# MLP turns by transfers, a scheduler with a backward pass, and another opening for head 0, in a retention and latent-attention decoder

## The chip, the cores and the metric

The kernel runs on one core of one Trainium2 chip. The metric is the time of one execution on the device in microseconds (us), as the median of three runs. One further execution was taken with the hardware profiler; every trace row below is from that one. The engines are named as the profile names them: PE (TensorE, the matrix products), PEld (its weight loads), DVE (VectorE), ACT (ScalarE), POOL (GpSimd) and SP (SyncE, which issues most of the transfers).

## The reference, cut to what matters

The input x has 256 tokens of 2048 features. One retention layer (8 heads, queries and keys of 256, gates and values of 512 columns) and one latent-attention layer follow each other, each with a squared-ReLU MLP of 8192 hidden columns behind it.

```python
h = rms_norm(x, norm_mix[0]);  x = x + retention(h, ret_w_in, ret_w_out, cos, sin)
x = x + square(relu(rms_norm(x, norm_mlp[0]) @ w1[0])) @ w2[0]
k_nope, k_pe, v = mla_shared_kv(rms_norm(x, kv_norm_in), ...)   # the latent: 2048 -> 512 + 64, then up
x = x + mla_attention(rms_norm(x, norm_mix[1]), ..., k_nope, k_pe, v)
x = x + square(relu(rms_norm(x, norm_mlp[1]) @ w1[1])) @ w2[1]
```

In a head of retention, `q` and `k` are rotated by cos and sin of the positions, `o = (q k^T * decay) v`, and `silu(gate) * o / rms(o)` goes into the output projection. All data is float32.

## The kernel before, in words

**Products.** Every float32 operand is split into a high part (rounded to float32r, by ACT, tiles `*_wh` for weights) and a low part (what is left, by DVE, `*_wl`), and a product is three matrix products: high x high, high x low, low x high. Weights are streamed in chunks of up to 1 MB into three `raw` buffers, issued by SP; the split tiles have five buffers each (`wh`, `wl`).

**Pairs.** Most projections go by `gemm_pair` (L812): two column blocks of 512 together, in chunks of 256 rows. A chunk is a 2 x 2 block product, done with eight block products (24 matrix products) or, where `kinds` says so, with seven (21), after the manner of Strassen. A seven-product chunk needs sums of weights and of activations, which DVE makes (`*_u`, `*_sum`, `*_more`). Tuples such as SEVEN, ODD, LATE and HEAD name the chunks with seven. A pair fills four accumulator banks (`acc`), two of tag `tp` and the double bank `at`; `pair_out` (L853) copies them out. Queries and keys go by `gemm_t` (L729), plain columns by `gemm` (L891).

**Turning.** The next product needs its input transposed, with the features on the partitions. Two ways exist. On PE: `transposed` (L649), a product of 128 columns with the identity for each 128 x 128 block, into a `tp` bank. By transfer: `turn_by_dma` (L660), where ACT copies each block's 16-bit halves apart (`*_h`), SP issues four transposing transfers per block pair (`*_t`), and `joined` (L676) puts the halves together on ACT.

**The MLP.** `mlp` (L1296) works in four groups. In a group, two up pairs (p even, p odd) make hidden blocks 0 to 3 and 4 to 7, then two down pairs (`d_.0`, `d_.1`) use these eight blocks as chunks 0 to 7. `up` scales and applies the ReLU (ACT), turns, squares (ACT) and splits. STEPS (L466) says how: blocks of the even pair are turned by transfer, those of the odd pair (`None`) on PE, in `turn_on_pe` (L1308). The even pair's blocks have the odd pair's time to get ready; the odd pair's blocks are used from the fifth chunk of the first down pair on.

**The opening.** Head 0 starts with its gate column (`rg`), then queries (`rq`), keys (`rk`) and its value column (`rv`), while x arrives block by block in `start` (L1119). POOL computes angles for the rotation in `sincos` (L995), one chain of 512 columns for retention (`tr`), one of 128 for the latent layer (`tm`); ACT takes the sine (`tr_sc`), DVE scales it by the tokens' rstd, and PE turns it (`tr_tp`) into `rope_tab`. All later heads do queries, keys and then gates and values as one pair (`rp`). The output projection `ro` comes in two halves, after heads 3 and 7; TURNED_Y (L463) says up to which head the results y are turned by transfer.

**Order.** The program is first recorded as a list of operations (`Plan`, L125), with times estimated by a table. `due_dates` (L229) goes back once over the dependencies, and `schedule` (L255) goes forward over the engines, taking on each the ready operation that is due first. Queue order on every engine, DMA issues included, comes from that. In every engine's queue the instructions start in that order: a waiting one holds those behind it.

Of the kernel before, what the change touches and what calls it, by code (L numbers as in the profile page):

```python
# [23 lines left out]

AHEAD = {"f2k": 25000, "act": 30000, "small": 60000}
# [99 lines left out]
class Plan:  # L125
# [129 lines left out]
    def schedule(self):  # L255
        import heapq

        self.due_dates()
        free = dict.fromkeys(self.LATENCY, 0.0)
# [7 lines left out]
        blocked = {t: {} for t in self.tags}  # L267
        for op in self.ops:
# [219 lines left out]
def yoco(ctx: ExitStack, tc: tile.TileContext, a):  # L488
# [49 lines left out]
    cst = nc.tile(pool, [P, C_ALL], F32, "cst")  # L538
# [3 lines left out]
    ident = cst[:, C_ID : C_ID + P]  # L542
    mask = cst[:, C_MASK : C_MASK + 3 * P]
# [8 lines left out]
    for i in range(9):  # L552
        nc.tensor.matmul(idle, zeros[:, 0:P], zeros, start=i == 0, stop=i == 8)
# [128 lines left out]
    def stream(w, chunk, cols, name, use, done=None, before=None):  # L682
# [5 lines left out]
        for half in range(2):  # L688
# [3 lines left out]
            if before is not None:  # L692
                cuts = 1 if half and chunk else 2
# [15 lines left out]
    def piece(w, chunk, acc, act, g, nk, nb, name, before=None, done=None):  # L709

        if before is None:
            need(act, 2 * g + 2)

        def use(half, wh, wl):
# [9 lines left out]
        stream(  # L724
            w, chunk, 4 * nb, f"{name}{g}", use, done and (lambda: done(acc)),
            before and (lambda half: before(2 * g + half)),
        )

    def gemm_t(w, chunk0, act, nk, name, done):  # L729
# [3 lines left out]
        for g in range(n):  # L733
            need(act, 4 * g + 4)

            def use(half, wh, wl):
                for j in range(4):
                    k = g * 8 + half * 4 + j
                    a = act[k // 2][:, k % 2]
                    for f in range(2):  # L740
                        cols = slice(j * 256 + f * P, j * 256 + (f + 1) * P)

                        def low():
                            nc.tensor.matmul(acc[f][:, 0:S], wl[:, cols], a[:, 0], start=False, stop=False)

                        if k > 0:
                            low()
                        nc.tensor.matmul(
                            acc[f], wh[:, cols], a.rearrange("p i s -> p (i s)"), start=k == 0, stop=k == nk - 1
                        )  # L750
                        if k == 0:
                            low()

            stream(w, chunk0 + g, 2048, f"{name}{g}", use, (lambda: done(acc)) if g == n - 1 else None)
# [136 lines left out]
    def gemm(w, chunk0, act, nk, nb, name, done, before=None):  # L891
# [3 lines left out]
        for g in range(n - 1):  # L895
            piece(w, chunk0 + g, acc, act, g, nk, nb, name, before)
        last_piece(w, chunk0, acc, act, nk, nb, name, done, before)

    def last_piece(w, chunk0, acc, act, nk, nb, name, done, before=None):
        g = nk // 4 - 1  # L900
        piece(w, chunk0 + g, acc, act, g, nk, nb, name, before, done)
# [143 lines left out]
    def mla_tables():  # L1045
        sm = mla_sc[0](no_turn[0])
# [14 lines left out]
    def ret_tables():  # L1061
        nc.vector.tensor_copy(pos_f, pos_i)
        ret_sc.append(sincos(cst[:, C_INVR : C_INVR + 128], 128, "tr"))

    def scale_tables():
# [3 lines left out]
        no_turn.append(zero)  # L1069
        sc = ret_sc[0](zero)  # L1070
        scaled = f2k([2, NT, P], "tr_scaled")
        for t in range(NT):
            nc.vector.tensor_scalar(scaled[:, :, t], sc[:, :, t], r0[t], None, op0=ALU.mult)
# [4 lines left out]
        later(1, turn)  # L1078


    act0, sums0, r0, ret_sc, mla_sc, no_turn = [], [], [], [], [], []
# [673 lines left out]
```

## Time and profile before

| | us |
|---|---|
| runs | 2434.78, 2441.07, 2440.16 |
| median | 2440.16 |
| profiled execution | 2433.66 |
| its span, first to last instruction | 2431.9 |
| PE, DVE, ACT, POOL busy | 2415.1, 2228.8, 1764.0, 251.7 |

A row of the chain or of the timeline gives the start, the duration, the engine, and what is done, with its count after the x. Where it ends in square brackets, the engine sat idle for that long before it, until the engine and tile named had finished. A group's row gives the busy time of the group, the mean of one in ns, and the idle time before them. A stretch gives busy time and count of each engine between two times, PE's clock, the busy share of the DMA engines and GB/s. In the names, what is written stands left of the arrow; the trace leaves buffer numbers out.

### The profile page before, as it was taken

The numbers are of one execution on the slowest core, as the hardware profiler recorded it, in microseconds if no ns is written. First come the engines' busy times: TensorE is split into PE (matmuls) and PEld (weight loads), VectorE is DVE, ScalarE is ACT, GpSimd is POOL, SyncE is SP. The second block draws the span as 40 slices with busy tenths as digits, with TensorE's granted clock in tenths as the row PEclk, the third lists the DMA queues.
The fourth block names the chain that finished last, engine by engine and source line by source line (L and its number), as shares of the span: only waits on it lengthen the run. The fifth ranks groups of instructions, "written<-read, shape, count | busy, mean of one in ns | idle before, by whom it ended". The sixth has DMA issues, their size and how long they took to land.

```text
span 2431.9 us, 31709 instructions
## 1 busy us (share of the span) xinstructions
PE 2415.1 (99%) x11342; PEld 2027.4 (83%) x11342; DVE 2228.8 (92%) x2959; ACT 1764.0 (73%) x2505; POOL 251.7 (10%) x287
## 2 busy tenths in 40 slices
PE   9999999999999999999999999999999999999998
PEld 7888888888888888888888888998888888888877
DVE  6899999988999999999999998777899999899999
ACT  6667666666687858769668879677878587596694
POOL 6510001000000010010110001110000100100100
PEclk9999999999999999999999999999999999999999
DMA  9566669656675697696896766545766986977984
GB/s 341 179 212 201 201 199 257 216 190 220 217 239 209 206 258 236 211 260 221 237 279 211 222 216 200 169 140 188 218 219 197 256 239 208 256 227 220 270 230 160
DMA packets 161151, 537.33 MB, mean 221 GB/s; under 512 B 78560, under 2 KB 79968, under 8 KB 107744
## 3 DMA queue, kind: packets, MB, share of 16 engines
q1 hardware_dynamic: 139600, 489.09, 60.9%
q0 software_dynamic: 21248, 46.15, 9.6%
q8 instruction: 89, 1.46, 0.2%
q14 instruction: 70, 0.57, 0.1%
q10 hardware_dynamic: 144, 0.05, 0.0%
HBM read 479.14 MB, written 39.85 MB: 213 GB/s over the span
## 4 chain that ended last, share of the span: by engine, by line
PE 76%; DVE 13%; ACT 5%; issue 4%; DMA 3%; SPq 0%; DVEq 0%; ACTq 0%
PE u_c L421 14%; PE d_c L421 12%; PE rp_c L421 8%; PE ro_c L421 5%; DVE d_wl L421 5%; PE u_p L421 4%; PE uq_acc L421 4%; PE rq_acc L421 4%; PE rk_acc L421 4%; PE d_p L421 3%; PE rp_p L421 3%; DVE d_u L421 2%; PE ku_acc L421 2%; DMA u_raw<-in_mlp_w 2%; DVE u_wl L421 2%
## 5 line engine op out<-in xcount | busy, mean ns | idle before, releaser
L421 PE MATMUL d_c<-d_wh,hid 128*128 128x512 f32 x1412 | 456.3, 390 | 0.0
L421 PE MATMUL u_c<-u_wh,n 128*128 128x512 f32 x1328 | 429.6, 389 | 0.0
L421 PEld LDWEIGHTS d_c<-d_wh,hid 128*128 128x128 f32 x1412 | 265.0, 188 | 54.6
L421 PEld LDWEIGHTS u_c<-u_wh,n 128*128 128x128 f32 x1328 | 249.3, 188 | 51.6
L421 DVE TENSOR_TENSOR d_wl<-d_raw,d_wh 128x1024 fp32r<-128x1024 f32 (+1 forms) x256 | 279.3, 1106 | 0.2 <-ACT d_wh L421 0.2
L421 ACT CAST u_wh<-u_raw 128x1024 fp32r<-128x1024 f32 (+1 forms) x256 | 236.6, 953 | 53.8 <-PE u_c L421 37.3
L421 PE MATMUL d_c<-d_wl,hid 128*128 128x512 f32 x706 | 274.8, 389 | 0.0
L421 DVE TENSOR_TENSOR u_wl<-u_raw,u_wh 128x1024 fp32r<-128x1024 f32 (+1 forms) x256 | 273.6, 1093 | 1.2 <-ACT u_wh L421 1.2
L421 PE MATMUL u_c<-u_wl,n 128*128 128x512 f32 x664 | 258.8, 390 | 2.6 <-DVE u_wl L421 2.5
L421 ACT CAST d_wh<-d_raw 128x1024 fp32r<-128x1024 f32 (+1 forms) x256 | 240.9, 967 | 19.9 <-PE d_c L421 8.0
L421 ACT CAST d_wh<-d_u 128x1024 fp32r<-128x1024 f32 x106 | 108.8, 1051 | 146.9 <-DVE d_u L421 139.4
L421 ACT CAST u_wh<-u_u 128x1024 fp32r<-128x1024 f32 x120 | 122.4, 1051 | 103.3 <-DVE u_u L421 93.5
L421 PE MATMUL rp_c<-rp_wh,a 128*128 128x512 f32 x560 | 180.8, 390 | 0.0
L421 PEld LDWEIGHTS d_c<-d_wl,hid 128*128 128x128 f32 x706 | 132.6, 188 | 27.2
L421 DVE TENSOR_TENSOR u_wl<-u_u,u_wh 128x1024 fp32r<-128x1024 f32 x120 | 143.1, 1219 | 12.3 <-ACT u_wh L421 12.3
L421 PEld LDWEIGHTS u_c<-u_wl,n 128*128 128x128 f32 x664 | 124.6, 188 | 30.0 <-DVE u_wl L421 4.3
L421 ACT CAST rp_wh<-rp_raw 128x1024 fp32r<-128x1024 f32 x112 | 103.7, 944 | 59.2 <-PE rp_c L421 33.4
L421 DVE TENSOR_TENSOR d_wl<-d_u,d_wh 128x1024 fp32r<-128x1024 f32 x106 | 126.9, 1218 | 14.5 <-ACT d_wh L421 14.3
L421 DVE TENSOR_TENSOR rp_wl<-rp_raw,rp_wh 128x1024 fp32r<-128x1024 f32 x112 | 119.4, 1092 | 6.3 <-ACT rp_wh L421 6.3
L421 PEld LDWEIGHTS rp_c<-rp_wh,a 128*128 128x128 f32 x560 | 105.1, 188 | 22.7 <-DVE rk_u L421 1.1
L421 PE MATMUL u_p<-u_wh,n_more 128*128 128x512 f32 x360 | 120.6, 389 | 0.0
L421 POOL DMA_DIRECT2D xh<-d_c x48 | 41.6, 866 | 736.8 <-DVE d_wl L421 536.1
(492 smaller groups left out, 6029.4 us busy)
## 6 DMA issues: line engine op xcount, KB each, us to landing
u_raw<-in_mlp_w SPq DMA_DIRECT2D x128, 1024.0 KB, 6.4
d_raw<-in_mlp_w SPq DMA_DIRECT2D x128, 1024.0 KB, 5.2
rp_raw<-in_ret_w_gv SPq DMA_DIRECT2D x56, 1024.0 KB, 5.1
ro_raw<-in_ret_w_out SPq DMA_DIRECT2D x32, 1024.0 KB, 5.1
uq_raw<-in_mla_w_uq SPq DMA_DIRECT2D x24, 768.0 KB, 4.1
rq_raw<-in_ret_w_qk SPq DMA_DIRECT2D x16, 1024.0 KB, 5.9
rk_raw<-in_ret_w_qk SPq DMA_DIRECT2D x16, 1024.0 KB, 4.9
xh<-d_c POOLq DMA_DIRECT2D x48, 256.0 KB, 6.2
```

Of the source, the lines that this page charges most:

```text
L421: op.made = fn(*(real(v) for v in op.args), **{k: real(v) for k, v in op.kw.items()})
```

## The change

- **MLP turns.** STEPS gives the odd up pairs the same steps by transfer as the even ones; `turn_on_pe` is no longer used. All up pairs take chunk 7 before chunk 6, and close their outputs one after another in the last chunk (`ends`).
- **Scheduler.** `schedule` now runs the forward pass up to six times. Between two passes, `latest` goes backward over the engines, one operation after another on each, and sets new due dates; the pass that ends first by the estimates is kept.
- **Head 0.** `gemm_two` computes queries and keys together while x arrives, 128 products; gates and values follow as a pair like those of other heads. The sums for its seven-product chunks are made from x as it arrives, in place of four further loads. x's blocks are loaded and copied to their home in DRAM beside that pair.
- **Tables.** One sine chain of 640 columns (`tab`) for both layers; the positions and frequencies come first, by ACT's queue.
- **Head 7** is turned by transfer too (TURNED_Y 8), and the second half of the output projection has three seven-product chunks in place of two (HALF).
- **Latent.** Its two column blocks go through the chunks in turn, not one after the other.
- Ten warm-up products instead of nine; stores of the second token half by ACT's queue.

MORE_HEAD is empty, so `more_sums` is not used; the other new keyword dictionaries are empty too.

```diff
+ROUNDS = 6
+    def latest(self):
...
+            op.due = free[e] = min(limit[op], free[e] - op.cost)
+            for other, finish in behind[op]:
+                gap = other.cost
+                if finish and not other.engine == op.engine == "PE":
+                    gap = (other.took if other.moves is None else gap + sum(other.moves)) + self.LATENCY[op.engine]
+                limit[other] = min(limit[other], op.due - gap)
...
     def schedule(self):
+        self.due_dates()
+        best = None
+        for _ in range(ROUNDS):
...
+                self.forward()
...
+            end = max(op.end for op in self.ops)
+            if best is None or end < best[0]:
+                best = (end, [(op.start, [b.slot for b in op.new]) for op in self.ops])
+            self.latest()
...
-TURNED_Y = 7
+TURNED_Y = 8
-STEPS = (((3,3,4),(3,4,5)),(None,None))
+STEPS = (((3,3,4),(3,4,5)),((3,3,4),(3,4,5)))
+MORE_FROM, MORE_HEAD, HALF = 5, (), (3,5,7)
...
+    nc.scalar.dma_start(pos_i, a["pos"])
+    nc.scalar.dma_start(inv, a["cst"][:, :C_MASK])
...
-    for i in range(9):
+    for i in range(10):
...
+    def gemm_two(w, act, nk, names, before, done):
+
+        acc = [accs(512, name) for name in names]
+        n = nk // 4
+        for g in range(n):
+            stream(
+                w, g, 2048, f"{names[0]}{g}", lambda half, wh, wl: four_t(acc[half], act, g * 4, nk, wh, wl),
+                (lambda: done(acc)) if g == n - 1 else None, lambda half: before(g) if half == 0 else None,
+            )
...
-        ret_sc.append(sincos(cst[:, C_INVR : C_INVR + 128], 128, "tr"))
+        turned_by.append(sincos(inv, C_MASK, "tab"))
...
+        u = f2k([2, S], f"x0s_{c}")
+        for j in range(2):
+            nc.scalar.activation(u[:, j], t[:, j], AF.Copy, scale=gains_of[j])
+        split_act(v, u)
+        later(1, lambda: sums0.__setitem__(c, with_sums(u, f"a0s_{c}")))
...
-            later(4 - b, lambda t=t, x0=x0: nc.gpsimd.dma_start(x_home[t][b], x0))
+            nc.gpsimd.dma_start(x_home[t][b], x0)
...
-                later(2 + b, lambda b=b: load_x(b))
-            later(6, scale_tables)
+                later(0.5 + b, lambda b=b: load_x(b))
+            later(5, scale_tables)
...
-            summed_up = len(y_act) in (HEAD if h < RH // 2 else LATE)
+            summed_up = len(y_act) in (HEAD if h < RH // 2 else HALF)
...
+        if h == 0:
+            gemm_two(a["ret_w_qk0"], act0, KD, ("rq0", "rk0"), start, lambda acc: (asked(acc[0]), keyed(acc[1])))
+            return
...
-            first = LATE if i else HEAD
+            first = HALF if i else HEAD
...
-            gemm(a["ret_w_gv0"], 0, act0, KD, 512, "rg0", gated, start)
...
-                    w1, p * 8, act, [i in seven for i in range(8)], f"u{layer}_{p}", lambda c, p=p, up=up: up(c, p)
+                    w1, p * 8, act, [i in seven for i in range(8)], f"u{layer}_{p}", lambda c, p=p, up=up: up(c, p),
+                    **(({"order": (0, 1, 2, 3, 4, 5, 7, 6), "ends": True}, {"order": (0, 1, 2, 3, 4, 5, 7, 6), "ends": True}))[p % 2],
...
-    for b in range(2):
-        gemm(a[f"mla_w_kv_down_{b}"], 0, act_kv, KD, KV_NBS[b], f"kd{b}", lambda acc, b=b: downed(acc, b))
+    kd = [accs(KV_NBS[b], f"kd{b}") for b in range(2)]
+    for g in range(KD // 4):
+        for b in range(2):
+            done = (lambda acc, b=b: downed(acc, b)) if g == KD // 4 - 1 else None
+            piece(a[f"mla_w_kv_down_{b}"], g, kd[b], act_kv, g, KD, KV_NBS[b], f"kd{b}", done)
...
-        nc.sync.dma_start(a["out"][t * P : (t + 1) * P, b * 512 : (b + 1) * 512], x[t][b])
+        (nc.sync, nc.scalar)[t].dma_start(a["out"][t * P : (t + 1) * P, b * 512 : (b + 1) * 512], x[t][b])
```

How the orders move, at three places. First ACT's queue at the beginning of the first down pair of group 1 in layer 0. `u_1` is the odd up pair, `hid_02` and `hid_03` are blocks of the even pair, `hid_10` to `hid_13` those of the odd pair, and `d_002`, `d_003` are the down pair's chunks 2 and 3. Before:

```order
L421 ACTIVATE u_1_c_7439<-u_1_c_7439,n_r 128x512
L421 COPY hid_02_u<-hid_01_t_7399 128x512
L421 CAST d_002_wh_7516<-d_002_raw 128x1024
L421 ACTIVATE hid_02_u<-hid_02_u 128x512
L421 ACTIVATE hid_10_u<-hid_10_tp 128x512
L421 ACTIVATE u_1_c_7443<-u_1_c_7443,n_r 128x512
L421 ACTIVATE hid_11_u<-hid_11_tp 128x512
L421 ACTIVATE u_1_c_7419<-u_1_c_7419,n_r 128x512
L421 CAST hid_02_7553<-hid_02_u 128x2x256
```

and now:

```order
L480 ACTIVATE u_1_c_7477<-u_1_c_7477,n_r 128x512
L480 COPY hid_10_h_7535<-u_1_c_7466 128x1024
L480 COPY hid_10_h_7543<-u_1_c_7477 128x1024
L480 CAST hid_02_7553<-hid_02_u 128x2x256
L480 COPY hid_03_u<-hid_01_t_7284 128x512
L480 CAST d_002_wh_7564<-d_002_raw 128x1024
L480 ACTIVATE hid_03_u<-hid_03_u 128x512
L480 CAST d_003_wh_7578<-d_003_raw 128x1024
L480 CAST d_003_wh_7587<-d_003_raw 128x512
L480 CAST hid_03_7593<-hid_03_u 128x2x256
L480 COPY u_1_p_7600<-u_1_p_7194 128x512
L480 COPY hid_10_u<-hid_10_t_7546 128x512
```

The square of a turned block straight from PE's bank (`hid_10_u<-hid_10_tp`) has given way to copies into halves (`hid_10_h`) and, ten rows later, the first copy back (`hid_10_u<-hid_10_t`), with weight casts between them.

Second, ACT's queue where the sine is taken. Before, among the casts of head 1's queries (`rq`):

```order
L421 CAST rq_wh_717<-rq_raw 128x1024
L421 ACT_TABLE_LOAD
L421 ACTIVATE tr_sc<-tr_rr,no_turn 128x512
L421 CAST rq_wh_740<-rq_raw 128x1024
L421 COPY rope_tab<-tr_tp 128x512
```

and now, in head 0's gate and value pair (`rp`), where the rows in front and behind are casts of its chunk 6 and then 7:

```order
L480 CAST rp_wh_662<-rp_raw 128x1024
L480 CAST rp_wh_670<-rp_raw 128x512
L480 ACT_TABLE_LOAD
L480 ACTIVATE tab_sc<-tab_rr,no_turn 128x640
L480 CAST rp_wh_707<-rp_u_683 128x1024
L480 CAST rp_wh_718<-rp_u_664 128x1024
L480 CAST rp_wh_733<-rp_raw 128x1024
```

The sine moved from between casts of a plain column to between the casts of one seven-product chunk.

Third, PE's queue at the latent, where the last two blocks of x are turned for it (`n_tp`, from `x_mlp`). The pair before these stands 24 rows ahead. Before:

```order
L421 MATMUL kd_acc_12742<-kd_wh_12749,n_20_12835 128x320
L421 MATMUL kd_acc_12752<-kd_wh_12749,n_20_12835 128x320
L421 MATMUL n_tp_12883<-cst,x_mlp_11686 128x128 x4
L421 MATMUL n_tp_12889<-cst,x_mlp_11686 128x128 x4
L421 MATMUL kd_acc_12752<-kd_wl_12793,n_20_12835 128x320
L421 MATMUL kd_acc_12752<-kd_wh_12749,n_20_12835 128x320
L421 MATMUL kd_acc_12742<-kd_wh_12771,n_21_12849 128x320
```

and now, 25 rows behind the pair before:

```order
L480 MATMUL kd_acc_12812<-kd_wh_12807,n_10_12798 128x320
L480 MATMUL kd_acc_12812<-kd_wl_12828,n_10_12798 128x320
L480 MATMUL n_tp_12941<-cst,x_mlp_11713 128x128 x4
L480 MATMUL n_tp_12949<-cst,x_mlp_11713 128x128 x4
L480 MATMUL kd_acc_12812<-kd_wh_12807,n_10_12798 128x320
L480 MATMUL kd_acc_12804<-kd_wh_12836,n_11_12843 128x320
L480 MATMUL kd_acc_12804<-kd_wl_12850,n_11_12843 128x320
```

The turns now stand between products of an earlier block of x (`n_10`, not `n_20`), at the same distance from the pair before them.

More of the change, by code (lines that the diff above doesn't have):

```diff
@@ L267, in schedule @@
         blocked = {t: {} for t in self.tags}
+        for op in self.ops:
+            op.ahead = []
         for op in self.ops:
@@ L692, in stream @@
             if before is not None:
-                cuts = 1 if half and chunk else 2
+                cuts = 1 if half or chunk else 2
                 m = n // cuts
@@ L707, in stream, with piece @@
             tick(0.5)
-    def piece(w, chunk, acc, act, g, nk, nb, name, before=None, done=None):
-        if before is None:
-            need(act, 2 * g + 2)
+    def piece(w, chunk, acc, act, g, nk, nb, name, done=None):
+        need(act, 2 * g + 2)
         def use(half, wh, wl):
@@ L1213, in turn @@
                 split_up(k2, u)
-        later(2 if h else 3, turn)
+        later(2, turn)
     ss = square_sums(NB, "ss1")
```

204 lines of the change are left out of this document (114 added, 90 removed).

## The prediction

> **What bounds the kernel now.** I read the page first, for shares and span, then the chain of work that ended last, then one group of the MLP as stretches.
>
> ```profile
> span 2431.9 us, 31709 instructions
> PE 2415.1 (99%) x11342; PEld 2027.4 (83%) x11342; DVE 2228.8 (92%) x2959; ACT 1764.0 (73%) x2505; POOL 251.7 (10%) x287
> PE 76%; DVE 13%; ACT 5%; issue 4%; DMA 3%; SPq 0%; DVEq 0%; ACTq 0%
> ```
>
> TensorE is busy for 99% of the span and carries the chain. So whatever removes products should shorten the run, as long as no other engine becomes late. DVE, at 92%, is the next one.
>
> ```profile
> 895.51 5.44 PE u_c L421 x24
> 905.71 5.44 PE u_c L421 x24
> ```
>
> These two pieces of the chain give the prices: 24 products of 512 columns take 5.44 us, so one takes 0.227 us. From one such piece to the next is 10.20 us, in which an eight-product chunk (24 products) and a seven-product chunk (21) are done: 5.44 and 4.76 us.
>
> ```profile
> core 0: us, PE busy (x) PEld busy (x) DVE busy (x) ACT busy (x) POOL busy (x), PEclk, DMA share, GB/s
> 885.30:926.10 40.80, 40.80 (x182) 33.78 (x181) 38.94 (x43) 25.47 (x31) 6.65 (x8) 1.00 0.91 261
> 926.10:966.90 40.80, 40.80 (x182) 33.78 (x181) 39.31 (x47) 35.53 (x48) 0.00 (x0) 1.00 0.73 230
> 966.90:1010.20 43.30, 43.30 (x201) 36.00 (x200) 43.19 (x58) 36.27 (x53) 0.00 (x0) 1.00 0.58 197
> 1010.20:1051.00 40.80, 40.80 (x182) 33.78 (x181) 38.38 (x42) 25.08 (x31) 7.18 (x9) 1.00 0.91 255
> ```
>
> The rows are the even up pair, the odd up pair, the first and the second down pair of group 2 in layer 0. Eight groups look alike. PE never rests. The third row decides: there DVE is busy for 43.19 of 43.30 us, and the odd pair's turns fall into it.
>
> **The change, part by part.** First the turns that leave TensorE: 128 products for the MLP.
>
> ```profile
> L421 PE MATMUL hid_tp<-cst,u_c 128*128 128x128 f32 x128 | 17.5, 274 | 1.5 <-ACT u_c L421 1.5
> 2016.84 1.03 PE L421 MATMUL hid_tp<-cst,u_c 128*128 128x128 f32 x8
> 2017.62 0.48 PE L421 MATMUL d_c<-d_wh,hid 128*128 128x512 f32 x1
> 2017.94 0.40 PE L421 MATMUL d_c<-d_wl,hid 128*128 128x512 f32 x1
> ```
>
> A block of eight turns takes 0.78 us from its start to the next product's, and that product then takes 0.32 instead of 0.227: 0.87 us. Sixteen blocks make 13.9 us, and the first row adds 1.5 us of waiting for ACT's relu. Head 7's eight turns (TURNED_Y) are another 0.9. The row's mean of 274 ns overlaps its neighbours, so I price by distance of starts. The Trainium skill ("TensorE: Matmul & The Clock Gate", Part 4: PE-mode transpose) gives about 275 ns for a transpose in one kernel's context. Our 274 ns agrees as a duration, but taken as a price it would make 35 us of the 128 turns and the sum about 20 us better; the starts contradict it.
>
> Products: head 0's gates and values took 192 products as two plain columns, and as a pair they take 4 x 24 + 4 x 21 = 180. HALF gives the second half of the output projection one more seven-product chunk in both pairs, 2 x 3 fewer. Together 18 x 0.227 = 4.1 us. **Removed on PE: 13.9 + 1.5 + 0.9 + 4.1 = 20.4 us.**
>
> What replaces the turns lies on ACT and SP:
>
> ```profile
> 775.16 1.98 ACT L421 COPY hid_h<-u_c 128x1024 uint16<-128x1024 uint16 x2
> 780.41 1.41 ACT L421 COPY hid_u<-hid_t 128x512 uint16<-128x512 uint16 x2
> L421 SPq DMA_TRANSPOSE hid_t<-hid_h x64: 1188/1226/2731, 776.2 to 2337.5; - x64
> DMA to landing us min/median/max: 2.4/3.4/6.9
> SPq L421 <- ACT hid_h L421: 44.1, 12, 4.5
> ```
>
> One odd pair needs 4 copies into halves (2 x 1.98) and 8 back (4 x 1.41): 9.6 us more ACT. The squares stay, only from SBUF. The order shows them all within the first down pair, since its chunks 4 to 7 use them. That stage has 36.27 us of ACT today, so 45.9, while PE's stage shrinks by two blocks to 41.55. The excess is 4.3 us per group. SP gets eight issues of 1.23 us there, and they hold weight loads behind them whenever ACT is late (12 such waits today, 3.7 us each); three raw buffers, some 15 us of products, cover that, and after them DVE would wait for weights, then PE. DMA has room (0.58 in that stage).
>
> Is ACT's excess paid by PE? From nothing, if the five wh tiles let ACT run ahead during the odd up pair (35.53 of 40.80 busy), to all 4.3. The nearest row is DVE's 43.19 of 43.30: an engine full for a whole stage cost PE nothing. So near zero, but not zero, since DVE too loses its 1.75 us there: I take 0.6 in each of 8 groups, **+4.8 us**. The new order of the up pairs (chunk 7 before 6, outputs closed one after another) starts ACT's copies earlier; I count that as what makes 0.6 possible. It also puts two seven-product chunks side by side, which is DVE's heavier kind.
>
> Head 7's blocks through the queue:
>
> ```profile
> 629.01 10.88 PE ro_c L421 x48
> 639.89 2.16 PE o L421 x9
> 647.29 0.74 DVE L421 SCALAR_TENSOR_TENSOR y<-o,o_r,rp_c 128x512 f32<-128x512 f32 x1
> L421 SPq DMA_TRANSPOSE y_t<-y_h x28: 1212/1322/2054, 121.6 to 608.0; - x28
> DMA to landing us min/median/max: 4.5/5.8/7.5
> ```
>
> The last y is ready at 648.0. Two copies (2.0), three further issues (4.0), landing (5.8), two copies and a cast (2.0) give 661.8. Chunk 6 of this projection starts at 629.0 + 4 x 5.44 + 2 x 4.76 + 2.2 = 662.5. It just fits; between 0 and 4 us late, I take **+1**.
>
> Head 0. Today the tables come late:
>
> ```profile
> 21.28 3.54 POOL L421 TENSOR_SCALAR tr_ang<-cst,pos_f 128x128 f32<-128x128 f32 x2 [20.44 <-DMA rg_raw<-in_ret_w_gv]
> 48.39 1.75 POOL L421 TENSOR_TENSOR n_r<-n_m,neg_half 128x2 f32<-128x2 f32 x1
> 51.39 1.20 POOL L421 TENSOR_SCALAR no_turn<-n_r 128x1 f32<-128x1 f32 x1
> 70.05 0.61 POOL L421 TENSOR_SCALAR tr_rr<-tr_rr 128x512 f32<-128x512 f32 x1
> L421 POOL DMA_DIRECT2D xh<-x x8: 563/596/780, 36.6 to 58.6; - x8
> 72.76 0.44 PE L421 MATMUL tr_tp<-cst,tr_scaled 128*128 128x128 f32 x2 [0.63 <-DVE tr_scaled L421]
> 6.16 1.22 PE L421 MATMUL rg_acc<-rg_wh,a 128*128 128x512 f32 x2 [0.96 <-ACT a L421]
> 6.16 24.13 PE rg_acc L421 x96
> 30.30 11.29 PE rq_acc L421 x64
> ```
>
> POOL's chain runs from 21.3 to 70.7; without eight issues (4.8) and the two rstd steps (3.0) it is 41.6 us of work. As one chain of 640 columns instead of 512 it is a quarter longer at most, 52 us, and with seven issues and those steps 59. It starts when the positions land, at about 6: ready at 65. The order now puts the sine in ACT's queue inside head 0's gate and value pair, in front of the last two casts of chunk 6, so those casts and every later one queue behind it. PE: 6.2, plus two columns at 11.3, plus 2 for the slow first products (the 96 of rg_acc took 24.1 us, 2.3 more than 96 x 0.227), starts the pair at 30.8 and chunk 6 at 62.1; nine of its products need none of those casts, to 64.1. Sine, cast and DVE's low part (0.9, 1.0, 1.2) end at 68.1. So up to 4 us, or 0 if the chain gains. x's loads and copies (4 MB) also move beside this pair, whose weights DVE needs sooner than those of queries and keys. Bounds 0 to 7, I take **+4**; the 0.63 above with its cast (0.8) goes, **-0.8**.
>
> The latent's columns in turn: the wait there is
>
> ```profile
> 1395.25 1.06 PE L421 MATMUL n_tp<-cst,x_mlp 128*128 128x128 f32 x8 [1.83 <-DVE n L421]
> ```
>
> It is the second pair of turned blocks waiting for a bank that ACT and DVE read in eight steps. The order keeps those steps and puts the second pair as close behind the first as before (25 rows later against 24), in front of the same latent products. So this edit brings 0; bounds -2 and +1.
>
> Edits with one answer, 0: the scheduler's two passes (they only redraw the orders, whose places are priced above), the second sine chain off POOL (nothing waits for it), positions and constants on ACT's queue, four re-reads of x gone, the tenth warm-up product (it runs before 6.16, where PE waits anyway), half of the stores on ACT's queue (-0.5 at best).
>
> Sum: -20.4 + 4.8 + 1 + 4 - 0.8 = **-11.4 us**. The trace was taken in an execution of 2433.66 us; the runs are 2434.78, 2440.16 and 2441.07. The mean of all four is 2437.4, so 2426.0. A measurement of this kernel can tell 0.3%, 7.3 us, from no change.
>
> **The rivals.** (1) *ACT becomes the bound in the first down pair.* For: 45.9 us of work in 41.55. Against: its slack in the stage before. It decides from 2.0 us per group for zero, and from 2.9 for slower by over 0.3%: the rest of the sum is -16.2. At 3.5 it gives 2437.4 - 16.2 + 28 = 2449. The Trainium skill ("VectorE: DVE Perf Modes", Rules for kernel authors) says the same: transpose 128x128 on TensorE if a PSUM destination will do, by DMA otherwise; here it did do. No run yet shows it either way. Chance 0.12.
>
> (2) *DVE is the bound behind PE.* A group holds 38.94 + 39.31 + 43.19 + 38.38 = 159.8 us of DVE in PE's 165.7, 164.0 afterwards. If PE's saving turns into waits for low parts, 1.8 us per group: 2437.4 - 16.2 + 14.4 = 2435.6, no change. Against: 4 us are left in each group. Chance 0.15.
>
> ```profile
> 1.18 4.02 PE L421 MATMUL idle<-zeros 128*128 128x512 bf16 x9 [1.18 <-DVE zeros L421]
> 2425.28 0.39 PE L421 MATMUL d_c<-d_wh,hid 128*128 128x512 f32 x1
> ```
>
> (3) *Everything is hidden.* No cost in the groups, at head 0 or head 7, and the new order also removes half of what PE waits today (16.8 us idle in the span, less the 1.2 and the 6.2 before its first and after its last product): 2437.4 - 21.2 - 4.7 = 2411.5. Chance 0.20.
>
> **How the numbers follow.** The forecast case keeps 0.53. It is faster by over 0.3% with 0.46, within with 0.06; (3) adds 0.20 to faster, (2) splits 0.03, 0.10 and 0.02, (1) gives 0.01 and 0.11 to same and slower. That makes 0.69, 0.17 and 0.14. The range takes in (3) and (2) and leaves most of (1) out: 2410 to 2441.
>
> **What would show it.** Right: no hid_tp on PE, 128 hid_t transposes on SP, ACT near 41 us in each first down pair, and PE's gaps there under 1 us; a wait for tab_sc or a cast behind it near 62 to 68 us; n_tp still waiting at the latent. Wrong: waits of d_c for d_wh or hid of 3 us per group would be (1); for d_wl with ACT idle, (2); a first down pair of 41.6 us in all eight groups, and a pair of head 0 without a gap, (3).

## The result and the profile after

The changed kernel takes 2455.38 us (median of 5 runs, 2450.31 to 2461.48), the kernel before 2438.68 in the same measurement (5 runs). The ratio is 1.0076, with a 95% interval of 1.0061 to 1.0091: the change made the kernel slower, by about 17 us, where I had forecast 2426.0 and faster, within 2410 to 2441.

First the page of the changed kernel, its span, its engines and the shares of the chain that ended last.

```profile
span 2459.7 us, 31582 instructions
PE 2416.6 (98%) x11189; PEld 2004.8 (82%) x11189; DVE 2269.2 (92%) x2993; ACT 1843.5 (75%) x2613; POOL 242.6 (10%) x262
PE 47%; DVE 23%; ACT 11%; issue 10%; DMA 8%; POOL 1%; SPq 0%; DVEq 0%; ACTq 0%; POOLq 0%
```

PE's busy time looks as before, with 153 products fewer. The chain tells more: PE's share fell from 76% to 47%, and DVE's rose from 13% to 23%. PE is waited for less and waits more.

Next, the four stretches of group 2 in layer 0, as the prediction showed them of before: even up pair, odd up pair, first and second down pair.

```profile
core 0: us, PE busy (x) PEld busy (x) DVE busy (x) ACT busy (x) POOL busy (x), PEclk, DMA share, GB/s
898.30:940.40 42.10, 41.75 (x182) 33.62 (x181) 40.74 (x44) 26.58 (x33) 6.90 (x8) 1.00 0.85 237
940.40:982.50 42.10, 41.41 (x181) 33.51 (x180) 41.30 (x50) 36.46 (x48) 0.00 (x0) 1.00 0.85 245
982.50:1024.10 41.60, 41.57 (x181) 33.35 (x180) 40.05 (x54) 40.99 (x60) 0.00 (x0) 1.00 0.67 218
1024.10:1065.70 41.60, 41.60 (x186) 34.41 (x184) 38.41 (x43) 26.76 (x34) 6.90 (x8) 1.00 0.87 255
```

The down pairs came out nearly as forecast: together 83.2 us, where 84.1 less 1.75 plus 0.6 makes 82.95, with ACT at 40.99 in the first. (The borders of the rows, here and in the prediction, are not quite those of the pairs. Counted by products, the first down pair took 42.6 us before and 41.7 now, so that 41.60 beside the forecast 41.55 is no proof by itself.) The surprise is in the first two rows. The two up pairs take 84.2 us where they took 81.6, with the same products. These are the rows for which the prediction had no term.

To see the whole, I cut both traces where the projection changes, and counted PE's gaps in each part. A gap is what lies between the starts of two neighbouring products beyond the 0.227 us of one, where it is more than 0.033. The last down pair is taken to the end of the span; 4.4 to 6.6 us of that lie behind the last product.

| part (us) | before: length, gaps | after: length, gaps | length |
|---|---|---|---|
| first warm-up product to head 1 | 74.6, 6.0 | 85.2, 17.7 | +10.6 |
| heads 1 to 3 | 228.7, 2.8 | 226.4, 0.4 | -2.3 |
| output projection, first half | 83.0, 0.1 | 84.3, 1.3 | +1.3 |
| head 4's pair | 40.9, 0.0 | 45.5, 4.5 | +4.6 |
| output projection, second half | 87.4, 0.2 | 85.0, 0.0 | -2.4 |
| MLP, all up pairs | 663.0, 4.0 | 686.7, 26.6 | +23.7 |
| MLP, all down pairs | 684.4, 3.7 | 676.0, 9.6 | -8.4 |
| latent | 29.8, 1.9 | 28.5, 0.9 | -1.3 |

The rest differs by 2 us together; the spans by 27.8. That is more than the 17 of the medians, since the profiled execution is the slowest of the five after and was the fastest before. How far one trace may be trusted was measured by accident (ends_only, below): two traces of one and the same program have MLP gaps of 39.8 and 28.3 us. So a sum of gaps is good to some 10 us, and I rest on what repeats.

The rows of PE's waits say for whom it waits. Columns: who waits, for what, us in total, times, longest. First before, then after.

```profile
PEld u_c L421 <- DVE u_wl L421: 4.3, 4, 2.6
DVE u_u L421 <- DMA u_raw<-in_mlp_w: 12.4, 15, 2.2
```

```profile
PEld u_c L480 <- DVE u_wl L480: 22.3, 29, 1.7
PEld u_p L480 <- DVE u_wl L480: 7.6, 6, 2.7
DVE u_u L480 <- DMA u_raw<-in_mlp_w: 21.4, 13, 3.5
```

In the up pairs PE waits for the low parts of weights, and DVE now and then for the weights. Of the 26.6 us of gaps 21.9 lie in the odd up pairs. A place shows it; DVE's timeline behind the end of an even up pair of the changed kernel (PE starts the odd pair at 1107.84), and the product that waits there:

```profile
1109.14 0.68 DVE L480 TENSOR_TENSOR u_u<-u_u,u_raw 128x512 f32<-128x512 f32 x1
1109.74 0.68 DVE L480 TENSOR_TENSOR u_u<-u_p,u_v 128x512 f32<-128x512 f32 x1
1110.35 0.68 DVE L480 TENSOR_TENSOR u_wl<-u_raw,u_wh 128x512 fp32r<-128x512 f32 x1
...
1114.99 1.23 DVE L480 TENSOR_TENSOR u_u<-u_raw 128x1024 f32<-128x1024 f32 x1 [1.62 <-DMA u_raw<-in_mlp_w]
1116.13 0.69 DVE L480 TENSOR_TENSOR u_v<-u_p,u_v 128x512 f32<-128x512 f32 x1
1116.73 1.22 DVE L480 TENSOR_TENSOR u_wl<-u_u,u_wh 128x1024 fp32r<-128x1024 f32 x1
```

```profile
1118.00 0.50 PE L480 MATMUL u_p<-u_wl,n_more 128*128 128x512 f32 x1 [0.94 <-DVE u_wl L480]
```

DVE works without a pause on the even pair's outputs and the odd pair's weights, then stands 1.62 us because the next weights have not landed, and has no reserve left: its low part ends at 1117.95, and PE takes it up at 1118.00.

### The profile page after: what moved, and what is told of

It is laid out like the page before. It is cut to its first block, busy times and chain, and to the rows that moved or that the text cites. A ratio compares the mean times of both kernels' runs of the same rounds, so it can differ in the third digit from the quotient of the medians.

```text
span 2459.7 us, 31582 instructions
## 1 busy us (share of the span) xinstructions
PE 2416.6 (98%) x11189; PEld 2004.8 (82%) x11189; DVE 2269.2 (92%) x2993; ACT 1843.5 (75%) x2613; POOL 242.6 (10%) x262
## 4 chain that ended last, share of the span: by engine, by line
PE 47%; DVE 23%; ACT 11%; issue 10%; DMA 8%; POOL 1%; SPq 0%; DVEq 0%; ACTq 0%; POOLq 0%
PE rp_c L480 8%; PE d_c L480 7%; DVE u_wl L480 7%; PE u_c L480 5%; PE uq_acc L480 4%; DVE d_wl L480 4%; PE rk_acc L480 3%; DMA u_raw<-in_mlp_w 3%; PE rp_p L480 3%; PE rq_acc L480 3%; ACT d_wh L480 3%; DVE u_u L480 2%; ACT hid_u L480 2%; PE d_p L480 2%; DVE d_u L480 2%
## 5 line engine op out<-in xcount | busy, mean ns | idle before, releaser
L480 PE MATMUL rp_c<-rp_wh,a 128*128 128x512 f32 x640 | 207.3, 390 | 2.0 <-DVE rk_u L480 1.2
L480 ACT CAST rp_wh<-rp_raw 128x1024 fp32r<-128x1024 f32 (+1 forms) x128 | 118.3, 944 | 68.9 <-PE rp_c L480 39.4
L480 DVE TENSOR_TENSOR rp_wl<-rp_raw,rp_wh 128x1024 fp32r<-128x1024 f32 (+1 forms) x128 | 137.5, 1099 | 8.1 <-ACT rp_wh L480 7.9
L480 PEld LDWEIGHTS rp_c<-rp_wh,a 128*128 128x128 f32 x640 | 120.1, 188 | 28.7 <-DVE rk_u L480 2.9
L480 PE MATMUL rp_c<-rp_wl,a 128*128 128x512 f32 x320 | 125.2, 391 | 3.4 <-DVE rp_wl L480 3.4
```

The costliest lines, as they stand in the source:

```text
L480: op.made = fn(*(real(v) for v in op.args), **{k: real(v) for k, v in op.kw.items()})
```

## The experiments

Theories for the MLP were four: the scheduler's backward pass, the chunk order, the transfers by way of SP's queue and DMA, and the transfers by way of ACT. For the opening there were two: POOL beside DVE, or simply more work on DVE. All times below are medians; each ratio is to runs of the kernel before on the same chip.

| kernel | us | ratio, 95% | to head 1 | up pairs: length, gaps | down pairs: length, gaps |
|---|---|---|---|---|---|
| before | 2438.7 | | 74.6 | 663.0, 4.0 | 684.4, 3.7 |
| after | 2455.4 | 1.0076 (1.0061-1.0091) | 85.2 | 686.7, 26.6 | 676.0, 9.6 |
| one_pass | 2463.0 | 1.0103 (1.0085-1.0120) | 85.1 | 674.8, 15.1 | 691.9, 25.5 |
| plain_up | 2459.7 | 1.0088 (1.0065-1.0111) | 84.8 | 666.2, 7.2 | 700.2, 32.6 |
| odd_on_pe | 2447.8 | 1.0040 (1.0026-1.0053) | 83.9 | 672.7, 13.0 | 679.1, 1.5 |
| before_two_way | 2439.7 | 1.0013 (1.0001-1.0024) | 73.8 | 671.7, 12.6 | 684.2, 4.9 |
| plain_pe | 2443.6 | 1.0032 (1.0018-1.0045) | 85.3 | 663.0, 4.0 | 685.4, 5.1 |
| old_head0 | 2435.4 | 1.0002 (0.9985-1.0020) | 74.0 | 667.1, 8.0 | 684.9, 6.3 |
| half_plain | 2438.2 | 1.0007 (0.9995-1.0019) | 87.8 | 661.0, 2.0 | 677.3, 5.8 |
| late_chain | 2451.3 | 1.0065 (1.0042-1.0088) | 86.7 | 674.6, 14.8 | 676.7, 10.2 |
| short_chain | 2444.3 | 1.0028 (1.0016-1.0040) | 75.6 | 681.1, 21.1 | 675.1, 8.5 |
| odd_no_square | 2448.2 | 1.0048 (1.0033-1.0064) | 87.4 | 667.5, 8.4 | 686.8, 19.8 |
| old_half | 2431.2 | 0.9984 (0.9968-0.9999) | 73.8 | 663.0, 3.8 | 683.8, 11.4 |
| old_half_one | 2461.3 | 1.0106 (1.0090-1.0123) | 75.5 | 664.4, 5.3 | 711.6, 39.1 |
| order_only | 2456.0 | 1.0085 (1.0064-1.0107) | 85.7 | 688.1, 28.2 | 671.7, 5.5 |
| ends_only | 2453.8 | 1.0080 (1.0057-1.0102) | 87.6 | 660.2, 1.4 | 694.7, 26.9 |
| half_short | 2433.0 | 0.9983 (0.9972-0.9994) | 75.2 | 663.7, 4.7 | 680.7, 9.0 |

### Which part of the change costs the MLP

**one_pass**

```diff
-ROUNDS = 6
+ROUNDS = 1
```

> The changed kernel with one forward pass of the scheduler, without the backward pass. Scheduler theory (the backward pass sets every due date as late as the engines allow, so DVE makes the low parts, and with them frees the raw buffers, without reserve): the gaps of the up pairs (26.6 us in the changed kernel, 4.0 in the one before) fall to about 5, and the time from 2455 to about 2434; the opening may gain too. Order theory (chunk 7 before 6, outputs closed one after another in the last chunk): nothing changes in the up pairs, 2455 within 5. Transfer theory (the odd pairs' turns by transfer crowd SP's queue and the DMA engines, so that weights arrive late): also 2455 within 5.

Measured 2463.0. The gaps do not go, they change place: fewer in the up pairs, 16 us more in the down pairs. The scheduler theory is out as the cause. The time lies above what any of the three theories gave.

**before_two_way**: the kernel before with `latest`, `forward` and the loop of `schedule`, nothing else of the diff.

> The kernel before with nothing but the scheduler's backward pass and its repeated forward passes. Scheduler theory: gaps of 2 to 4 us in each up pair appear here too, 2439 + 20 = about 2459, or at least over 2446. Order theory and transfer theory: no gaps, 2439 within 5.

2439.7, 0.13% above before (0.01 to 0.24%). Its up pairs have gaps of 12.6 us in this trace, 10.4 of them in the last group of each layer, far from the 2 to 4 in each pair that the theory asked for.

**plain_up**

```diff
-                    **(({"order": (0, 1, 2, 3, 4, 5, 7, 6), "ends": True}, {"order": (0, 1, 2, 3, 4, 5, 7, 6), "ends": True}))[p % 2],
```

> The changed kernel with the up pairs' chunks in plain order, their outputs closed as before. Order theory: the gaps of the up pairs fall from 26.6 to about 5 us, 2455 to about 2434; the first down pairs may lose some, since the copies of the outputs start later. Scheduler theory: up pairs keep their gaps, 2455 within 5. Transfer theory: the same, 2455 within 5.

2459.7. The up pairs do lose their gaps, as the order theory said, and the time does not fall: the down pairs' gaps rise from 9.6 to 32.6. Here PE waits for something else.

```profile
PEld d_c L480 <- ACT hid L480: 20.6, 17, 3.4
```

```profile
976.11:1021.72 45.61, 42.32 (x181) 33.05 (x180) 42.12 (x57) 43.29 (x63) 0.00 (x0) 1.00 0.64 206
1012.72 0.69 ACT L480 CAST hid<-hid_u 128x512 fp32r<-128x512 f32 x1
...
1016.24 1.05 ACT L480 CAST d_wh<-d_u 128x1024 fp32r<-128x1024 f32 x1 [2.32 <-DVE d_u L480]
```

The first row is the largest of plain_up's waits of PE in the MLP, the second its first down pair of group 2 as a stretch, the others are from ACT's timeline there: the high part of the last hidden block, and the only idle time of ACT in the stage. Seventeen waits for the high part of a hidden block, which ACT makes. ACT is at work for 43.29 us in a stage whose products take 41.1 without their gaps, and it pauses only after the last block is done. So the new order did not make the loss; it moved it from one stage to another.

**odd_on_pe**

```diff
-STEPS = (((3,3,4),(3,4,5)),((3,3,4),(3,4,5)))
+STEPS = (((3,3,4),(3,4,5)),(None,None))
```

> The changed kernel with the odd up pairs' blocks turned on TensorE again, everything else as changed. Transfer theory: the up pairs lose their gaps (minus 22 us), the 128 turns and their wait come back (plus 15.4) and the down pairs' own gaps go (minus 6): about 2442. Order theory and scheduler theory: the gaps of the up pairs stay, the turns come back, less the down pairs' gaps: 2455 + 15.4 - 6 = 2464.

2447.8: with 128 turns back on PE the kernel is 8 us faster. The transfers cost more than the turns that they replace. The transfer theory had 2442, the others 2464, and the up pairs keep about half of their gaps: 13.0, against 4.0 in plain_pe. That looks like the order's own price, but it is one trace each, and the intervals of the two ratios overlap.

**plain_pe** has both edits, plain order and turns on PE.

> The changed kernel with the up pairs in plain order and the odd pairs' blocks turned on TensorE: its MLP is then that of before. Theory now (neither order pays: the turns by transfer fill ACT in the first down pair, and the other order only moves that lack into the up pairs): the gaps of the MLP fall from 36.2 us (32.6 + 7.2 in plain order with transfers) to about 8, and the time is the one before plus what the opening loses (10.6) less what heads 1 to 3, the output projection and the latent gain (6): 2438 + 5 = about 2443. If the scheduler or the opening shifts something in the MLP too: over 2447.

2443.6, as expected. (32.6 and 7.2 make 39.8, not the 36.2 written there.) The MLP is that of before again, so the rest of the loss lies ahead of it.

### Why the transfers cost

**half_plain**: plain order, and of each odd pair's two column blocks only the second goes by transfer.

```diff
-STEPS = (((3,3,4),(3,4,5)),((3,3,4),(3,4,5)))
+STEPS = (((3,3,4),(3,4,5)),(None,(3,4,5)))
```

> The changed kernel with plain up order, the odd pairs' first column block turned on TensorE and the second by transfer: half of ACT's extra 9.6 us in the first down pair, half of SP's eight issues. ACT theory: ACT has 41.1 us of work in a stage of 42.4, the down pairs' gaps fall from 32.6 to about 8, the turns of one block come back (7.7): about 2443, a little below plain_pe or level with it. Queue theory (transposes hold weight loads behind them on SP): the gaps go by half only, to about 16, and the time stays near 2450.

2438.2, below what either theory gave. The down pairs' gaps fall from 32.6 to 5.8, not to half: that speaks for a full engine and against a queue whose delays add up. PE's waits for ACT's `hid` have gone from the list, and the MLP takes 1338.3 us, 9 less than before (2 of them behind the last product).

**odd_no_square** leaves the squares of the odd pairs out, in plain order.

```diff
-                    nc.scalar.activation(u, u, AF.Square)
+                    if p % 2 == 0:
+                        nc.scalar.activation(u, u, AF.Square)
```

> The changed kernel with plain up order, in which the squares of the odd pairs' hidden blocks are left out: four steps of about 0.6 us fewer on ACT in each first down pair, and nothing else; the transfers, their issues and DVE's work stay. ACT theory (ACT is full there, 41 of 41.6 us): the down pairs' gaps fall from 32.6 us by up to 2.5 us per group, to 13 to 20, and the time from 2459.7 to about 2445. Queue theory (the transposes on SP hold the weight loads back): the gaps stay near 32 and the time near 2460.

2448.2, and the gaps fall to 19.8. The same wait as in plain_up's row, in this kernel:

```profile
PEld d_c L480 <- ACT hid L480: 11.2, 8, 1.7
```

All 128 transposes and their issues are still there, only ACT has less to do, and 9 us of waits for it are gone. This wait repeats well: the second trace of plain_up's program (ends_only) has 20.5 us of it. So it is ACT, not SP's queue. The edit also takes one step out of the chain of each block; whether the load or the chain's length counts, it does not tell.

**order_only** and **ends_only** split the new order of the up pairs.

```diff
-                    **(({"order": (0, 1, 2, 3, 4, 5, 7, 6), "ends": True}, {"order": (0, 1, 2, 3, 4, 5, 7, 6), "ends": True}))[p % 2],
+                    order=(0, 1, 2, 3, 4, 5, 7, 6),
```

> The changed kernel with chunk 7 before chunk 6 in the up pairs, but their outputs closed as before. If the two seven-product chunks side by side (DVE's heavier kind) make DVE late: the up pairs keep most of their 26.6 us of gaps, over 18. If the closing one after another is the cause: they fall to 5 to 10, and the down pairs' gaps rise from 9.6 towards the 32.6 of plain order. In both cases the time stays within 2452 to 2462.

2456.0, with 28.2 us of gaps in the up pairs: the chunk order does it, the other way of closing the outputs does nothing that can be seen. PE waits there as in the changed kernel, while DVE itself waits for weights less than before the change (12.4):

```profile
PEld u_c L480 <- DVE u_wl L480: 17.5, 20, 1.3
DVE u_u L480 <- DMA u_raw<-in_mlp_w: 8.7, 9, 2.1
```

In plain_up it is the other way round, 18.6 us of such waits of DVE and 7.2 of gaps. So the up pairs are late without late weights, and weights land late without much delay of the up pairs: they are not the cause, though in the changed kernel they may add to it.

> The changed kernel with the up pairs' chunks in plain order, but the outputs closed one after another in the last chunk, which then is a seven-product chunk and closes as before whatever is asked, unless it has eight: chunk 7 is among the seven-product ones, so this should do nothing, and the result should be that of plain_up: up gaps near 7, down gaps near 32, 2460 within 4. If the two differ by more, the difference is what the placing of the same work by the scheduler or the chip alone can do.

As expected the closing has no effect in plain order: the program is plain_up's, the same instructions in the same order on every engine. It measured 2453.8 against 2459.7, further apart than the 4 us expected, and 28.3 us of MLP gaps against 39.8. The ratios, 1.0080 and 1.0088, agree within their intervals.

### The opening

In the changed kernel PE waits in the opening for DVE's low parts of x. PE's timeline:

```profile
20.36 0.50 PE L480 MATMUL rq_acc<-a,rq_wh 128*128 128x512 f32 x1 [0.54 <-DVE a L480]
...
25.70 0.50 PE L480 MATMUL rq_acc<-a,rq_wh 128*128 128x512 f32 x1 [1.60 <-DVE a L480]
...
28.53 0.50 PE L480 MATMUL rq_acc<-a,rq_wh 128*128 128x512 f32 x1 [1.16 <-DVE a L480]
```

The group of those low parts (ns: min/median/max, then first and last start), before and after:

```profile
L421 DVE SCALAR_TENSOR_TENSOR a<-x0t,gains,a x16: 476/479/483, 6.3 to 22.1; 128x256 fp32r<-128x256 f32 x16
```

```profile
L480 DVE SCALAR_TENSOR_TENSOR a<-x0t,gains,a x8: 474/934/1825, 6.9 to 28.4; 128x256 fp32r<-128x256 f32 x8
```

The same instruction on the same shape takes up to 3.8 times as long. POOL's and DVE's timelines of the changed kernel, side by side, say why:

```profile
16.75 1.57 POOL L480 TENSOR_TENSOR tab_kl<-tab_k,tab_kh 128x640 f32<-128x640 f32 x1
18.28 1.74 POOL L480 TENSOR_TENSOR tab_rr<-tab_ang,tab_part 128x640 f32<-128x640 f32 x1
20.11 1.87 POOL L480 TENSOR_SCALAR tab_part<-tab_kl 128x640 f32<-128x640 f32 x1
22.06 1.58 POOL L480 TENSOR_TENSOR tab_rr<-tab_rr,tab_part 128x640 f32<-128x640 f32 x1
```

```profile
16.77 3.53 DVE L480 SCALAR_TENSOR_TENSOR a<-x0t,gains,a 128x256 fp32r<-128x256 f32 x2
20.23 0.80 DVE L480 TENSOR_TENSOR a0s_sum<-x0s,a0s_sum 128x128 f32<-128x128 f32 x1
20.95 1.21 DVE L480 TENSOR_TENSOR rq_wl<-rq_raw,rq_wh 128x1024 fp32r<-128x1024 f32 x1
22.09 1.83 DVE L480 TENSOR_TENSOR a0s_sum<-x0s 128x256 f32<-128x256 f32 x1
```

POOL's first step starts at 16.75, DVE's at 16.77, and the two low parts last until 20.30, 0.28 us behind POOL's second step (20.02). The sum at 22.09 ends at 23.92, again 0.28 behind POOL's (23.64); alone such a sum takes 0.42. The Trainium skill ("SBUF — State Buffer", Who interferes with whom) says that a VectorE operation with two SBUF inputs contends with a GpSimd operation that reads SBUF, and calls the port pair that the two share an exclusive lock. Beside POOL's two-input steps shown the trace agrees: DVE ends 0.28 us behind POOL each time. Beside a one-input step (20.11 to 21.98) it agrees in part: the sum at 20.23 takes 0.80 us where 0.28 do alone, but it ends long before POOL's step, and the low part of weights behind it, at 20.95, takes 1.21 us, as it does where POOL rests.

**late_chain** starts POOL later.

```diff
-    nc.scalar.dma_start(pos_i, a["pos"])
-    nc.scalar.dma_start(inv, a["cst"][:, :C_MASK])
...
-        if g == 0:
-            first_tables()
...
         if g == 3:
+            nc.sync.dma_start(pos_i, a["pos"])
+            nc.sync.dma_start(inv, a["cst"][:, :C_MASK])
+            first_tables()
```

> The changed kernel with positions and frequencies loaded behind x and the weights on SP's queue, so that POOL starts the sine chain some 13 us later. Contention theory (while POOL runs its two-input steps, DVE's low parts of x take 1.8 us instead of 0.47, and DVE has no pause in 9.6 to 43): the opening, 7.6 to 38.6 now, ends near 33; of these 5 us some come back where the tables are late, so 2450 to 2455. Load theory (DVE has simply more to do there, the sums of x): the opening ends at 38 or later, and the time is 2455 or more.

Its low parts of x:

```profile
L480 DVE SCALAR_TENSOR_TENSOR a<-x0t,gains,a x8: 477/480/481, 5.4 to 21.2; 128x256 fp32r<-128x256 f32 x8
```

They are back at 480 ns. As stretches, queries and keys, then head 0's pair:

```profile
5.90:33.90 28.00, 24.93 (x128) 21.54 (x129) 23.70 (x38) 21.80 (x37) 11.67 (x6) 0.88 0.95 350
33.90:87.90 54.00, 46.56 (x181) 36.31 (x180) 49.13 (x44) 29.55 (x47) 44.28 (x30) 0.91 0.64 217
```

Queries and keys end at 33.9 in place of 38.6. But the pair, now beside POOL (44.28 us busy), takes 54.0 us instead of 47.7, so that head 1 starts no earlier. The cost moved along with the chain. The time, 2451.3, is within the expected range, though not for this reason: the trace has its gain in the MLP, within what a trace can scatter.

**short_chain** leaves most of the range reduction out (`r` is the angle less `k` times one constant; of POOL's 25 steps for the tables 9 are left).

> The changed kernel with most of the sine chain's range reduction left out (one step in place of seven, so the angles are less exact): POOL's work in the opening falls from some 45 us to about 15 and ends near 25. Contention theory: DVE's steps take their undisturbed times from there on, the tables are ready before head 0's pair asks for them, and head 1 begins at 77 to 80 instead of 86; the time is 2446 to 2449. Load theory (DVE's own extra work, the sums of x, is what is late): head 1 begins at 85 or later, 2454 or more.

2444.3, a little below the range, and head 1 begins at 76.8. These are the opening and head 0's pair as stretches, of the changed kernel and of this one.

```profile
7.60:38.60 31.00, 26.60 (x129) 21.63 (x130) 29.72 (x38) 21.89 (x38) 27.55 (x15) 0.89 0.80 292
38.60:86.30 47.70, 43.24 (x184) 33.34 (x183) 43.34 (x53) 29.46 (x47) 24.60 (x20) 1.00 0.69 251
```

```profile
6.50:34.70 28.20, 25.39 (x129) 21.29 (x130) 25.51 (x39) 22.65 (x38) 11.70 (x11) 0.88 0.93 339
34.70:76.80 42.10, 41.25 (x182) 33.30 (x181) 35.93 (x58) 28.36 (x45) 5.29 (x8) 1.00 0.75 275
```

With POOL's busy time down from 52 to 17 us (DMA issues included), DVE's for much the same work falls from 73.1 to 61.4, though its sums of x are all still there. That decides between the two theories: POOL's chain costs the opening its time.

**old_head0** goes the other way: before's opening and MLP with the rest of the change.

> The kernel before with the scheduler's passes, head 7 turned by transfer with HALF, the latent's columns in turn and the stores on two queues; the opening and the MLP are those of before. Against plain_pe it differs by the opening alone. If the opening is what loses: 2438 - 2.4 - 1.3 = about 2434, and its trace reaches head 1 about 10 us earlier than plain_pe. If the opening's loss comes back later (heads 1 to 3 end 2.4 us earlier behind it): the two differ by 8.

2435.4; it is 8 us below plain_pe, which differs from it by the opening and its tables alone. In the traces the opening is 11.3 us shorter, and 4 are given back in the up pairs.

### Versions that beat both

**old_half** is old_head0 with half_plain's STEPS.

> The opening and the plain order of before, with the scheduler's passes, head 7 by transfer and HALF, the latent in turn, and the odd pairs' second column block alone turned by transfer. If the parts add up: old_head0's 2435 less what half_plain's MLP gains over plain_pe's (1348.4 to 1338.3, 10): 2425, faster than before by 0.5 per cent. If the half turns paid only beside the new opening's delays or the parts collide: 2432 or more.

2431.2, ratio 0.9984 (0.9968 to 0.9999): a little below before, 6 us short of the sum of the parts.

**old_half_one** is the same with ROUNDS = 1.

> The same with one forward pass, without the backward pass. The backward pass put gaps of 3 to 7 us into the last up pairs of both layers where it was added alone (before_two_way), though not beside the half turns in half_plain. If the single pass has the better order: 2420 to 2424. If the passes pay or do nothing: 2425 or more.

2461.3, a miss of 40 us against the better of the two expectations. Its largest wait of PE in the MLP:

```profile
PEld d_c L480 <- ACT hid L480: 24.9, 8, 3.9
```

Eight waits, one per group, of 3.1 us. ACT has hardly more work than in old_half; the first down pair of group 2 there, and then here:

```profile
964.60:1007.76 43.16, 42.84 (x188) 34.40 (x189) 43.01 (x58) 39.91 (x58) 0.00 (x0) 1.00 0.66 209
```

```profile
970.61:1015.13 44.52, 42.14 (x189) 34.37 (x188) 44.52 (x60) 40.49 (x59) 0.00 (x0) 1.00 0.61 201
```

ACT does 58 instructions in the one and 59 in the other, and is idle for 4 us of the second stage. The copies into halves begin 18.0 us into the stage in old_half and 22.0 here, and PE then waits 2.38 us for the block's high part. So it is ACT's order, not its load alone. With half of the turns by transfer the passes are worth 30 us, on the changed kernel 8, on the kernel before nothing.

**half_short** takes both causes away from the changed kernel: half_plain's edits and the short chain.

> Both causes taken away at once from the changed kernel: plain up order with one block of two turned on TensorE (half_plain, 2438.2), and the short sine chain, with most of the range reduction left out (short_chain, 11 us below the changed kernel). If the two losses are separate they add: 2438 less 10 is about 2428, below the kernel before by 0.3 per cent or more. If the opening's gain is given back later (short_chain lost 3 us more than the changed kernel in head 4's pair): 2433 or more.

2433.0, ratio 0.9983 (0.9972 to 0.9994), below before but 5 us above the sum. In the trace the opening gives its 12.6 us, while heads 1 to 3 lose 3.3 and the MLP 6 against half_plain. So the two causes account for the loss, but their removal does not add up in full.

## Why the prediction was wrong, point by point

1. **What leaves PE, -20.4: right.** Without their gaps, and up to the last product's start, the down pairs went from 674.1 to 661.0 us, by 13.1 for the 13.9 of sixteen blocks. (The table's lengths give 14.3, but 1.2 of that lie behind the last product.) The second output projection gave 2.4, for 0.9 of turns and 1.4 of products. Pricing a turn by distance of starts held.
2. **The MLP's cost, +4.8: this step failed.** The 0.6 per group came true for the stage that it was written for: the gaps of the first down pairs rose by 3.3 us, 0.4 per group, those of all down pairs by 5.9, 0.7 per group. Of the 9.6 us that I put on ACT there, 4.7 came in that stage (36.27 to 40.99), 8.4 in the whole group. What failed is the sentence behind it: that the new order "starts ACT's copies earlier; I count that as what makes 0.6 possible", and that it "also puts two seven-product chunks side by side, which is DVE's heavier kind". I named that cost and gave it no price. It was 22.6 us in the trace, 2.8 per group, waits of `u_c` for `u_wl`. In plain order the cost shows where I looked for it: 26.9 and 32.6 us of gaps in the down pairs, some 3.3 per group more than before. That is rival (1), which I had priced at 3.5 per group and given 0.12. Rival (1) had the cause, rival (2) the place where it showed (waits for low parts), at a higher price than its 1.8.
3. **Why it was held unlikely.** I took DVE's 43.19 of 43.30 us as the row that shows a full engine costing PE nothing. For ACT it did not hold: in plain order it had 43.3 us of work in a stage of 41.1 us of products, and PE's weight loads waited 20 us for it in all. That DVE's full stage consists of weights, which can be prepared ahead, and ACT's of a chain of steps for a block that is due at the fifth chunk, is my explanation; no run separates it.
4. **Head 0, +4 - 0.8, and 2.7 of products: mis-sized, +0.5 where +10.6 was measured.** I followed POOL's chain only to the moment when its table is ready, and bounded that. Its cost beside DVE, from 6.5 us on, had no term, and the opening up to 38.6 was put down at its full rate. A wait near 64 came (1.8 us, at 66.1), but for a low part of DVE's that took 2.5 us beside POOL, not for a cast behind the sine; that one, at 69.5, held nothing that PE waited for before 82. short_chain gives 9.6 of the 10.6 back. The trace of before had the sign already. These are DVE's low parts in it, before POOL's chain began and during it, and POOL's step there:

```profile
17.68 1.23 DVE L421 TENSOR_TENSOR rg_wl<-rg_raw,rg_wh 128x1024 fp32r<-128x1024 f32 x1
39.87 2.85 DVE L421 TENSOR_TENSOR rk_wl<-rk_raw,rk_wh 128x1024 fp32r<-128x1024 f32 x1 [1.60 <-ACT rk_wh L421]
40.32 1.30 POOL L421 TENSOR_TENSOR tr_rr<-tr_rr,tr_part 128x512 f32<-128x512 f32 x1
```

5. **Head 7, +1:** none of it was seen. **Latent, 0:** -1.3. Heads 1 to 3 lost 2.3 us of gaps that I had not counted on.
6. **Scheduler, 0:** right for the kernel before (+0.13%), wrong beside transfers: with half of the turns they decide 30 us.
7. **Open:** head 4's pair, +4.6. DVE waits there for weights; the pair takes 42.3 to 48.6 us in the kernels with the new opening and 40.8 to 43.8 in those with the old one. No run took it apart. Open is also why the new order makes DVE late in the up pairs: it happens without weights that land late (order_only), and that two seven-product chunks side by side are too much for DVE at once fits, but was not measured by itself.

## What to carry to other kernels

Work taken from the bounding engine has to be put through every other engine's budget by stage, and an engine that becomes full in a stage is the new bound unless its work there can be done ahead: in plain order, half of the turns by transfer took 9 us off the MLP, and all of them added 8 and 19 in two traces of the same program. A reordering that removes a wait must be priced where it puts the load next, not only where it takes it away; gaps counted by stage show this at once. When a background chain is started earlier, look at who works beside it, not only at when it ends.

## What the runs showed of the hardware

In the changed kernel's opening, three low parts and a sum of DVE's, all with two inputs in SBUF, stood still until a two-input step of POOL had ended (0.48 us became 1.8). Where DVE's operation had started first, POOL's step stretched instead: 2.52 us at 25.67 and 5.57 at 33.44, for the 1.56 of the same step at 42.45. Beside one-input steps DVE's operations took 0.53 us longer at most (0.28 became 0.80), and some lost nothing (1.21 stayed 1.21). A chain of 47 us on an engine that is 10% busy cost the kernel 10 us that way. And one program, run twice, can differ by 6 us in its median and by 11 in the gaps of its traces, with ratios to the kernel before that agree.
